# Two-level Strassen products in four stretches instead of two, with a ring of seven weight places

## The chip, the cores and the metric

The kernel runs on one core of a Trainium2 chip. The metric is the device time of one execution in microseconds (us). Lower is better.

## What is computed

One layer of a decoder trunk on 1024 tokens of width 1024, all in fp32, with two branches that share one input projection, and a final norm:

```python
h = rms_norm(x, norm_mix_g[i])
proj = jnp.einsum('bsd,dc->bsc', h, w_in[i])
(q, k, v, z_a, gk_low, cb, cc, xc, z_c, g_a, g_c) = jnp.split(proj, idx, axis=-1)
gk = jax.nn.log_sigmoid((jnp.einsum('bsr,rk->bsk', gk_low, w_gk2[i]) + b_gk[i])) / GATE_NORMALIZER
o = gla_chunked(q, k, v, gk)                       # by heads; causal gated linear attention
o = rms_norm(o, gla_norm_g[i])
y_a = jnp.einsum('bsv,vd->bsd', o * jax.nn.silu(z_a), w_branch_a[i])
u = causal_dwconv(cc * xc, conv_w[i])
y_c = jnp.einsum('bsc,cd->bsd', (cb * u) * jax.nn.silu(z_c), w_branch_c[i])
merged = jax.nn.sigmoid(g_a + b_ga) * y_a + jax.nn.sigmoid(g_c + b_gc) * y_c
x = x + jnp.einsum('bsd,de->bse', merged, w_out[i])
ple_gate = jax.nn.sigmoid(jnp.einsum('bsd,de->bse', rms_norm(x, norm_ple_g[i]), w_ple_gate[i]))
x = x + ple_gate * jnp.einsum('bsq,qd->bsd', p[i], w_ple_proj[i])
return rms_norm(x, norm_final_g)
```

q and k have 512 columns each; v, z_a, cb, cc, xc, z_c, g_a and g_c have 1024. The change touches how the projections q, k, cc, xc, z_c and cb are multiplied.

## The kernel before, in words

**Arithmetic.** Every fp32 operand is split into a high part, rounded by a ScalarE copy, and a low part, the difference that VectorE subtracts (`split`, line 598). A product of two such operands takes three matmuls, high x high, high x low and low x high (`mm3`, line 609).

**First level.** A `Cell` (line 738) is 256 columns of a weight against all 1024 tokens, cut into 2 x 2 blocks of 512 tokens or inner rows and 128 columns. It is computed with seven block products instead of eight (Strassen's scheme in Winograd's form; products 0 to 6). A first-level product is 12 matmuls of 128 x 512 into one PSUM bank. Its banks are called X, Y and V (`bank`, line 635); X holds product 0, and a copy of X by ScalarE is the seed of Y, so that product 2 adds to it. V holds product 1. The left operand of a product, the prepared weights, lies in one place of a ring of `RING` places (tiles whi and wlo); the right operand is one of seven resident sums of h (`hres`, tiles h0 to h6, high and low).

**Second level.** A `Deep` (line 855) takes two Cells a and b, whose names join to the name of its tiles (`cc2xc20` is the Deep of cc2 and xc2 for first-level product 0). It computes first-level product k (0 or 1) of both Cells together by a second seven-product scheme. Each of these second-level products is six matmuls of 128 x 256 into one half of a bank of a or b (`product`, line 900), 42 in all in place of 2 x 24 of that width. There are 17 Deeps: for k = 0 of two pairs of q and k (q0/k0, q1/k1) and eight conv pairs (cc/xc, zc/cb in four groups), and for k = 1 of seven conv pairs. `prep` (line 872) makes their weights: the sums s1 to s4 of columns of a and b, then four places of the ring by `put`: A (a11 and a12), S (s1, s2), T (s3, s4) and B (a22). The right operands are quarters of h0 (k = 0) or h1 (k = 1), and four quarter sums, "turned", that are loaded from DRAM (tqd) by `quarters` (line 1679).

**How a Deep ran.** In two stretches (`run`, line 909). The first: products 2, 1, 4 and 0, 24 matmuls, into b left, b right, a right and a left. Behind it ScalarE copies b left into a tile `dw`, VectorE adds a left to it, writes b right + dw into b left, adds a right to dw, ScalarE copies dw into a right, and VectorE adds dw to b right. The second stretch, 18 matmuls, adds products 6, 3 and 5 to b left, a left and a right. Then for k = 0 the bank becomes the Cell's X, and for k = 1 its V; for pairs that have no Deep for k = 1, and for those of k = 1, Y is then taken and seeded by a copy of X.

**What sets the order.** `line_up` (line 943) writes the order of the first-level products by hand and inserts the stretches of the Deeps between them, so that about one first-level product or more stands between two stretches of one Deep. `run_groups` (line 972) walks through this list and looks ahead: it loads weights for up to RING + 6 places and prepares them for up to RING - 1. The joint products of v and z (`joint`, line 1294; j0, j1) and the rest of these projections (`rest_of`, line 1334; tiles vY, vX) put their operands in the same ring. Work beside the products (weights of the later layers, gates) is woven in: a generator advances by `tick`, which the products call. `weights` (line 1375) loads pieces of the two later weights (tile wt), scales those of the second by a vector on ScalarE, forms the four differences of the scheme on VectorE (128 x 256 each) and stores them.

Everything is recorded by a class `Flow`, given due times from TensorE's order backwards (`set_dues`, line 373), listed per engine with a cost model (`put_in_order`, line 420), and emitted from one place, so that all instructions carry line 508 in the profile and are told apart by their tiles. TensorE follows the written order of the products; VectorE's, ScalarE's, GpSimd's and SyncE's (SP's) orders come from the list.

Of the kernel before, what the change touches and what calls it, by code (L numbers as in the profile page):

```python
# [9 lines left out]
F32 = mybir.dt.float32  # L10
# [4 lines left out]
ALU = mybir.AluOpType  # L15

P = 128
# [5 lines left out]
CH = 64  # L23
NP = HALF // P
EPS = 1e-6
RING = 8

# [490 lines left out]
def kernel(  # L520
# [16 lines left out]
    nc = Flow(tc)  # L537
    PS = bass.MemoryType.PSUM
    tt = nc.vector.tensor_tensor
# [95 lines left out]
    def bank(cell, n):  # L635
        return psm.tile([P, 512], F32, tag=f"m{3 * cell.set + n}", name=f"{cell.name}{'XYV'[n]}")
# [218 lines left out]
    class Deep:  # L855
# [53 lines left out]
        def run(self, k):  # L909
            self.prep(k)  # L910
            a, b = self.pair
            left, right = slice(0, 256), slice(256, 512)
            if k == 0:
                self.a, self.b = bank(a, 2 * self.k), bank(b, 2 * self.k)
                self.product(2, self.b[:, left], True)
                self.product(1, self.b[:, right], False)
                self.product(4, self.a[:, right], True)
                self.product(0, self.a[:, left], False)
                d = self.pool.tile([P, 256], F32, tag="dw", name=f"{a.name}{self.k}dw")
                nc.scalar.copy(d, self.b[:, left])  # L920
                tt(d, self.a[:, left], d, op=ALU.add)
                tt(self.b[:, left], self.b[:, right], d, op=ALU.add)
                tt(d, self.a[:, right], d, op=ALU.add)
                nc.scalar.copy(self.a[:, right], d)
                tt(self.b[:, right], self.b[:, right], d, op=ALU.add)
            else:
                self.product(6, self.b[:, left], False)
                self.product(3, self.a[:, left], False)
                self.product(5, self.a[:, right], False)
                for c, t in ((a, self.a), (b, self.b)):  # L930
                    if self.k:
                        c.V = t
                        c.c22 = c.taken("s5", t)
                    else:
                        c.X = t
                    if c.prods[1] == 5:
                        if c.Y is not None:
                            c.join()
                    elif self.k or 1 not in c.deep:
                        c.Y = bank(c, 1)  # L940
                        nc.scalar.copy(c.Y, c.X)

    def line_up(groups):
        for n, g in enumerate(groups):
            for s, c in enumerate(g):
                c.set = (s if len(g) > 1 else n) % 2
        todo = []
        for g in groups:
            own = [(g[s], k) for s, k in (g[0].order or [(s, k) for k in g[0].prods for s in range(len(g))])]
            if g[0].deep and g[0].prods[1] == 5:  # L950
                own.insert(3, (g[0].deep[0], 0))
                own.insert(6, (g[0].deep[0], 1))
            elif g[0].deep and 1 not in g[0].deep:
                todo.insert(len(todo) - 1, (g[0].deep[0], 0))
                own.insert(1, (g[0].deep[0], 1))
            elif g[0].deep:
                at = len(todo)
                g[0].deep[1].behind = [(c, j) for c, j in todo[-2:] if j == 6]
                for m, (k, n, left) in enumerate(((0, 0, 5), (0, 1, 3), (1, 0, 2), (1, 1, 0))):
                    todo.insert(at - left + m, (g[0].deep[k], n))  # L960
            todo += own
        return todo

# [113 lines left out]
    with phase("prep0") as pool:  # L1077
# [86 lines left out]
        at = [0]  # L1164
# [210 lines left out]
    def weights(pool, some, pace, hurry):  # L1375


        def soon(do, *a, **kw):
            nc.hurry = hurry
            do(*a, **kw)  # L1380
            nc.hurry = 0.0

        for w, kt, cs in some:
            t = pool.tile([P, 4, 256], F32, tag="wt", name=f"wt{w}_{kt}_{cs.start}")
            soon(load, t, wb[w][:, :, kt, cs].rearrange("n p c -> p n c"))
            yield pace
            b11, b12, b22, b21 = (t[:, n] for n in range(4))
            if w:
                for n, q in enumerate((b11, b12, b22, b21)):
                    k = kt + 4 * (n >= 2)  # L1390
                    soon(act, q, q, AF.Copy, scale=gple[:, k:k + 1])
                    if n != 1:
                        soon(store, wtd[w][4 + (n + 1) // 2][:, kt, cs], q)
            soon(tt, b11, b12, b11, op=ALU.subtract)
            yield 1
            soon(tt, b12, b22, b12, op=ALU.subtract)
            yield 1
            soon(tt, b22, b22, b11, op=ALU.subtract)
            yield 1
            soon(tt, b21, b21, b22, op=ALU.subtract)  # L1400
            for n, q in enumerate((b11, b22, b12, b21)):
                soon(store, wtd[w][n][:, kt, cs], q)
            yield 2
# [816 lines left out]
```

## Time and profile before

| | |
|---|---|
| median of 3 runs | 1067.74 us (1067.62 to 1067.81) |
| profiled execution, its own time | 1068.09 us |
| its span in the trace | 1066.3 us |
| instructions in the span | 15934 |
| mean granted TensorE clock | 0.998 |
| moved by DMA | 254.72 MB, mean 239 GB/s |

The profile shows one execution. Its time of 1068.09 us holds the span of 1066.3 us, first to last instruction, and 1.8 us around it. PE is TensorE, PEld its weight loads, DVE is VectorE, ACT is ScalarE, POOL is GpSimd, SP is SyncE, which issues the DMAs. In a row of the timeline the first number is the start in us, the second the duration; a bracket at the end holds the time that the engine waited before it, and for whom. In a list of waits the numbers are the sum in us, the count and the mean. In a table of windows each engine's busy time stands with its instructions, in the order PE, PEld, DVE, ACT, POOL, then the granted clock, the share of DMA and GB/s (after the window and its length).

### The profile page before, as it was taken

The numbers are of one execution on the slowest core, as the hardware profiler recorded it, in microseconds if no ns is written. First come the engines' busy times: TensorE is split into PE (matmuls) and PEld (weight loads), VectorE is DVE, ScalarE is ACT, GpSimd is POOL, SyncE is SP. The second block draws the span as 40 slices with busy tenths as digits, with TensorE's granted clock in tenths as the row PEclk, the third lists the DMA queues.
The fourth block names the chain that finished last, engine by engine and source line by source line (L and its number), as shares of the span: only waits on it lengthen the run. The fifth ranks groups of instructions, "written<-read, shape, count | busy, mean of one in ns | idle before, by whom it ended". The sixth has DMA issues, their size and how long they took to land.

```text
span 1066.3 us, 15934 instructions
## 1 busy us (share of the span) xinstructions
PE 1057.2 (99%) x5163; PEld 894.8 (84%) x5163; DVE 929.3 (87%) x1578; ACT 672.3 (63%) x1264; POOL 46.5 (4%) x83
## 2 busy tenths in 40 slices
PE   9999999999999999999999999999999999999997
PEld 7888888888888888888888888988888888888886
DVE  6899859978997889889879799996999879889896
ACT  6867859895544545656456488875856534466555
POOL 0000000000000000000000011110000000012021
PEclk9999999999999999999999999999999999999999
DMA  8997368866865544653644759868695779799953
GB/s 317 336 353 260 136 218 278 308 230 223 268 186 207 189 158 144 222 178 133 217 154 159 245 177 311 269 238 303 217 314 208 286 223 310 247 319 341 310 217 145
DMA packets 163331, 254.72 MB, mean 239 GB/s; under 512 B 14384, under 2 KB 75568, under 8 KB 160304
## 3 DMA queue, kind: packets, MB, share of 16 engines
q1 hardware_dynamic: 163104, 253.45, 70.0%
q8 instruction: 40, 0.66, 0.3%
q14 instruction: 43, 0.35, 0.1%
q10 hardware_dynamic: 144, 0.26, 0.1%
HBM read 165.58 MB, written 88.08 MB: 238 GB/s over the span
## 4 chain that ended last, share of the span: by engine, by line
PE 92%; ACT 2%; DVE 2%; DMA 2%; issue 0%; SPq 0%; POOL 0%; POOLq 0%; ACTq 0%
PE vY L508 3%; PE pe L508 2%; PE op L508 2%; PE j0Y L508 1%; PE j1X L508 1%; PE j0X L508 1%; PE j0V L508 1%; PE kv L508 1%; ACT L508 1%; DMA k0raw<-in_wc_dram 1%; PE ga1Y L508 1%; PE ga3Y L508 1%; PE k0Y L508 1%; PE cc3Y L508 1%; PE ga0Y L508 1%; PE cc2Y L508 1%
## 5 line engine op out<-in xcount | busy, mean ns | idle before, releaser
L508 ACT ACT_TABLE_LOAD x25 | 32.1, 1283 | 1.1 <-PEq L2209 0.7
L508 DVE TENSOR_TENSOR wt<-wt 128x256 f32<-128x256 f32 x64 | 27.1, 423 | 1.2 <-DMA ccd<-c 0.5
L508 ACT ACTIVATE junk<-x 128x512 bf16<-128x512 f32 (+1 forms) x30 | 18.0, 600 | 12.2 <-DVE x L508 11.9
L508 DVE SCALAR_TENSOR_TENSOR u<-t,vec,u 128x512 f32<-128x512 f32 x32 | 24.1, 753 | 0.1
L508 POOL MEMSET t<- 128x2 f32 x8 | 0.8, 99 | 399.6 <-ACT kk L508 192.9
L508 POOL TENSOR_SCALAR rg<-ms 128x1 f32<-128x1 f32 x8 | 6.4, 796 | 263.0 <-ACT junk L508 262.9
L508 ACT ACTIVATE wt<-wt,vec 128x256 f32<-128x256 f32 x32 | 13.9, 499 | 1.5 <-DMA cb2raw<-in_wc_dram 1.0
L508 ACT ACTIVATE u<-t,vec 128x512 f32<-128x512 f32 x16 | 11.6, 724 | 5.1 <-DVE t L508 4.7
L508 ACT ACTIVATE junk<-op 128x256 bf16<-128x256 f32 x32 | 12.3, 383 | 3.3 <-PE op L508 3.1
L508 ACT ACTIVATE og<-op,or 128x256 f32<-128x256 f32 x32 | 13.4, 470 | 1.0 <-POOL or L508 1.0
L508 ACT ACTIVATE oq<-oq,vec 128x512 f32<-128x512 f32 x20 | 13.2, 714 | 0.0
L508 PE MATMUL op<-v,aTh 128*128 128x256 f32 x64 | 12.8, 283 | 0.0
L508 PE MATMUL pe<-wpelo,pThi 128*128 128x512 f32 x32 | 12.8, 400 | 0.0
L508 PE MATMUL pe<-wpehi,pThi 128*128 128x512 f32 x32 | 12.7, 396 | 0.0
L508 DVE TENSOR_TENSOR s<-y,s 128x512 f32<-128x512 f32 x16 | 11.0, 687 | 1.5 <-ACT s L508 1.0
L508 POOL TENSOR_SCALAR or<-oms 128x2 f32<-128x2 f32 x16 | 6.4, 400 | 135.1 <-ACT junk L508 135.1
L508 POOL TENSOR_TENSOR or<-or,mhalf 128x2 f32<-128x2 f32 x16 | 12.2, 764 | 1.3
L508 PE MATMUL pe<-wpehi,pTlo 128*128 128x512 f32 x32 | 12.1, 394 | 0.0
L508 DVE TENSOR_TENSOR x<-x,pe 128x512 f32<-128x512 f32 (+1 forms) x18 | 11.3, 631 | 0.4
L508 DVE TENSOR_TENSOR szl<-og,szl 128x512 f32<-128x512 f32 x16 | 11.0, 686 | 0.5 <-ACT og L508 0.5
L508 DVE STREAM_TRANSPOSE oT<-szl 128x512 f32<-128x512 f32 x16 | 11.3, 707 | 0.0
L508 DVE SCALAR_TENSOR_TENSOR hq<-hq,vec,rt 128x512 f32<-128x512 f32 x16 | 11.3, 745 | 0.0
(4072 smaller groups left out, 4353.5 us busy)
## 6 DMA issues: line engine op xcount, KB each, us to landing
wtd<-wt SPq DMA_DIRECT2D x88, 128.0 KB, 2.4
wt<-in_wb_dram SPq DMA_DIRECT2D x16, 512.0 KB, 4.2
wgq<-wtd SPq DMA_DIRECT2D x7, 1024.0 KB, 7.4
vraw<-in_wv_dram SPq DMA_DIRECT2D x24, 256.0 KB, 4.4
zraw<-in_wv_dram SPq DMA_DIRECT2D x20, 256.0 KB, 3.7
uq<-ud SPq DMA_DIRECT2D x5, 1024.0 KB, 7.5
oq<-od SPq DMA_DIRECT2D x5, 1024.0 KB, 6.3
qk<-qkd SPq DMA_DIRECT2D x12, 384.0 KB, 5.1
```

The source lines that it names most:

```text
L508: o.call(*[place(a) for a in o.args], **{k: place(a) for k, a in o.kw.items()})
```

## The change

The Deep runs in four stretches: product 0; products 4 and 2; product 1; products 3, 5 and 6. Product 0 goes into a left, and ScalarE copies it into b left. Product 2 adds to this copy by TensorE, and product 1 adds to the sum. Between them ScalarE copies b left to a tile dw0 and a right to a tile dw1, and VectorE adds dw0 to a right. After product 1 VectorE writes b left + dw1 to b right. So two additions of 256 columns by VectorE and three copies by ScalarE (seed, dw0, dw1) stand where there were four additions and two copies. For k = 1 the seed of Y by a copy of X moves ahead of the last stretch. `line_up` puts one first-level product between two stretches of a Deep; where a pair has Deeps for both k, the last stretch of k = 0 and the first of k = 1 stand together. The ring has seven places instead of eight, which also shortens the reach of `run_groups` by one. In `weights`, two subtractions of 256 columns become one of 512; the woven order goes on by two steps behind it, as it did behind the two.

```diff
@@ -23,7 +23,7 @@
-RING = 8
+RING = 7
@@ -912,21 +912,26 @@
             left, right = slice(0, 256), slice(256, 512)
             if k == 0:
                 self.a, self.b = bank(a, 2 * self.k), bank(b, 2 * self.k)
-                self.product(2, self.b[:, left], True)
-                self.product(1, self.b[:, right], False)
-                self.product(4, self.a[:, right], True)
-                self.product(0, self.a[:, left], False)
-                d = self.pool.tile([P, 256], F32, tag="dw", name=f"{a.name}{self.k}dw")
-                nc.scalar.copy(d, self.b[:, left])
-                tt(d, self.a[:, left], d, op=ALU.add)
-                tt(self.b[:, left], self.b[:, right], d, op=ALU.add)
-                tt(d, self.a[:, right], d, op=ALU.add)
-                nc.scalar.copy(self.a[:, right], d)
-                tt(self.b[:, right], self.b[:, right], d, op=ALU.add)
+                self.product(0, self.a[:, left], True)
+                nc.scalar.copy(self.b[:, left], self.a[:, left])
+            elif k == 1:
+                self.product(4, self.a[:, right], False)
+                self.product(2, self.b[:, left], False)
+                self.d = [self.pool.tile([P, 256], F32, tag=f"dw{n}", name=f"{a.name}{self.k}dw{n}") for n in range(2)]
+                nc.scalar.copy(self.d[0], self.b[:, left])
+                nc.scalar.copy(self.d[1], self.a[:, right])
+                tt(self.a[:, right], self.a[:, right], self.d[0], op=ALU.add)
+            elif k == 2:
+                self.product(1, self.b[:, left], False)
+                tt(self.b[:, right], self.b[:, left], self.d[1], op=ALU.add)
+                if self.k:
+                    for c in self.pair:
+                        c.Y = bank(c, 1)
+                        nc.scalar.copy(c.Y, c.X)
             else:
-                self.product(6, self.b[:, left], False)
                 self.product(3, self.a[:, left], False)
                 self.product(5, self.a[:, right], False)
+                self.product(6, self.b[:, left], False)
                 for c, t in ((a, self.a), (b, self.b)):
                     if self.k:
                         c.V = t
@@ -936,7 +941,7 @@
                     if c.prods[1] == 5:
                         if c.Y is not None:
                             c.join()
-                    elif self.k or 1 not in c.deep:
+                    elif 1 not in c.deep:
                         c.Y = bank(c, 1)
                         nc.scalar.copy(c.Y, c.X)
 
@@ -948,16 +953,19 @@
         for g in groups:
             own = [(g[s], k) for s, k in (g[0].order or [(s, k) for k in g[0].prods for s in range(len(g))])]
             if g[0].deep and g[0].prods[1] == 5:
-                own.insert(3, (g[0].deep[0], 0))
-                own.insert(6, (g[0].deep[0], 1))
+                for n, m in enumerate((3, 5, 7, 9)):
+                    own.insert(m, (g[0].deep[0], n))
             elif g[0].deep and 1 not in g[0].deep:
-                todo.insert(len(todo) - 1, (g[0].deep[0], 0))
-                own.insert(1, (g[0].deep[0], 1))
+                at = len(todo)
+                for n in range(3):
+                    todo.insert(at - 3 + 2 * n, (g[0].deep[0], n))
+                own.insert(1, (g[0].deep[0], 3))
             elif g[0].deep:
                 at = len(todo)
                 g[0].deep[1].behind = [(c, j) for c, j in todo[-2:] if j == 6]
-                for m, (k, n, left) in enumerate(((0, 0, 5), (0, 1, 3), (1, 0, 2), (1, 1, 0))):
+                for m, (k, n, left) in enumerate(((0, 0, 5), (0, 1, 4), (0, 2, 3), (0, 3, 2), (1, 0, 2), (1, 1, 1), (1, 2, 0))):
                     todo.insert(at - left + m, (g[0].deep[k], n))
+                own.insert(1, (g[0].deep[1], 3))
             todo += own
         return todo
 
@@ -1391,10 +1399,8 @@
                     soon(act, q, q, AF.Copy, scale=gple[:, k:k + 1])
                     if n != 1:
                         soon(store, wtd[w][4 + (n + 1) // 2][:, kt, cs], q)
-            soon(tt, b11, b12, b11, op=ALU.subtract)
-            yield 1
-            soon(tt, b12, b22, b12, op=ALU.subtract)
-            yield 1
+            soon(tt, t[:, 0:2], t[:, 1:3], t[:, 0:2], op=ALU.subtract)
+            yield 2
             soon(tt, b22, b22, b11, op=ALU.subtract)
             yield 1
             soon(tt, b21, b21, b22, op=ALU.subtract)
```

How the instructions stand, at three places. In these rows every instruction carries line 508; operation, written and read tiles and the shape follow.

TensorE around the first Deep, q0/k0 (q0V is a bank of the Cell q0; k0X and q0X are the two banks of the Deep, turned0 the loaded quarter sums of h0, and q0k00 with A or S its weights), before:

```order
L508 MATMUL q0V<-h5hi,q0lo 128x512
L508 MATMUL k0X<-turned0h,q0k00Shi 128x256
L508 MATMUL k0X<-turned0l,q0k00Shi 128x256
L508 MATMUL k0X<-turned0h,q0k00Slo 128x256
L508 MATMUL k0X<-turned0h,q0k00Shi 128x256
```

and now:

```order
L508 MATMUL q0V<-h5hi,q0lo 128x512
L508 MATMUL q0X<-h0hi,q0k00Ahi 128x256
L508 MATMUL q0X<-h0lo,q0k00Ahi 128x256
L508 MATMUL q0X<-h0hi,q0k00Alo 128x256
L508 MATMUL q0X<-h0hi,q0k00Ahi 128x256
```

The Deep began with a product that reads the loaded sums; it begins with product 0, which reads a quarter of h0.

ScalarE ahead of the joint of the v products (j1c and j1V: results and banks of the joint product j1; v_1hi, v_2hi: high halves of operands of v; vY: banks of the next product), before:

```order
L508 CAST v_1hi<-vraw_1_1269 128x512
L508 COPY j1V_1396<-j1c_1451 128x512
L508 CAST v_2hi<-vraw_2_1274 128x512
L508 COPY j1V_1404<-j1c_1457 128x512
L508 COPY j1c_1553<-j1Y_1394 128x512
```

and now:

```order
L508 CAST v_1hi<-vraw_1_1274 128x512
L508 COPY j1V_1386<-j1c_1442 128x512
L508 COPY j1c_1548<-j1Y_1384 128x512
L508 COPY j1c_1552<-j1Y_1391 128x512
L508 COPY vY_1559<-j0c_1015 128x512
```

With one place fewer, the cast v_2hi and the copy of the second j1V stand behind the copies of j1Y.

ScalarE in the pair cc2/xc2 (cb1, zc1: Cells before it; s_0_1: a gate; wt: later weights; cc2X, xc2X: the banks of the Deep; cc20dw: its dw), before:

```order
L508 CAST cb1hi<-cb1T_4813 128x512
L508 CAST zc1hi<-zc1T_4633 128x512
L508 ACTIVATE s_0_1_4933<-zc1u_4818 128x512
L508 COPY cc20dw<-xc2X 128x256
L508 CAST cb1hi<-cb1T_4664 128x512
L508 ACTIVATE wt_1_0_4901<-wt_1_0_4901,vec 128x256 x4
L508 COPY cc2X<-cc20dw 128x256
```

and now:

```order
L508 CAST cb1hi<-cb1T_4833 128x512
L508 COPY xc2X<-cc2X 128x256
L508 ACTIVATE s_0_1_4913<-zc1u_4758 128x512
L508 CAST zc1hi<-zc1T_4622 128x512
L508 COPY cc20dw_4946<-cc2X 128x256
L508 CAST cb1hi<-cb1T_4637 128x512
L508 COPY cc20dw_4957<-xc2X 128x256
```

The second copy waited for a VectorE addition; now three copies wait for TensorE alone, and the scaling of wt stands behind them.

## The prediction

> **What bounds the kernel now.** I read the page first, then the waits of TensorE, then the timeline of TensorE at the places that the waits name, then the stretch that the change touches.
>
> ```profile
> span 1066.3 us, 15934 instructions
> PE 1057.2 (99%) x5163; PEld 894.8 (84%) x5163; DVE 929.3 (87%) x1578; ACT 672.3 (63%) x1264; POOL 46.5 (4%) x83
> PE 92%; ACT 2%; DVE 2%; DMA 2%; issue 0%; SPq 0%; POOL 0%; POOLq 0%; ACTq 0%
> ```
>
> TensorE is busy for 1057.2 of 1066.3 us, and the chain that ended last runs over it for 92%. A busy TensorE can still hide waits, since matmuls overlap in the records, so the list of its own waits counts for more:
>
> ```profile
> PE warm L508 <- DVE zero L508: 1.0, 1, 1.0
> PE q0X L508 <- DMA turned0l<-tqd_0l: 0.3, 1, 0.3
> PE vY L508 <- ACT vY L508: 0.2, 1, 0.2
> ```
>
> That is the whole list: 1.0 us at the start and two waits later. The last matmul starts here:
>
> ```profile
> 1058.40 0.28 PE L508 MATMUL gt3Z<-wg6hi,gt3lo 128*128 128x256 f32 x1
> ```
>
> It ends at 1058.7, so the tail behind TensorE is 7.6 us. The order of its last rows on VectorE and ScalarE is unchanged, so I price it at nothing. The stretch that the change rewrites lies within 238 to 590 us:
>
> ```profile
> 290.00:590.00 300.00, 300.00 (x1619) 260.88 (x1619) 264.33 (x512) 162.51 (x326) 1.35 (x10) 1.00 0.54 178
> ```
>
> TensorE is busy for all 300 us of it, at the full granted clock (1.00), VectorE for 264 (88%), ScalarE for 163 (54%). So work taken off VectorE is taken off an engine that TensorE does not wait for. What can be gained is the two waits; what can be lost is any new wait in 17 products, or TensorE's own handling of a finer cut. A measurement of this kernel tells about 0.2%, 2.1 us, from no change.
>
> **What leaves VectorE.**
>
> ```profile
> 445.86 0.42 DVE L508 TENSOR_TENSOR cc20dw<-cc2X,cc20dw 128x256 f32<-128x256 f32 x1
> 446.19 0.42 DVE L508 TENSOR_TENSOR cc2xc21S<-xc2T 128x256 f32<-128x256 f32 x1
> 446.52 0.43 DVE L508 TENSOR_TENSOR xc2X<-xc2X,cc20dw 128x256 f32<-128x256 f32 x1
> L508 DVE TENSOR_TENSOR wt<-wt 128x256 f32<-128x256 f32 x64 | 27.1, 423 | 1.2 <-DMA ccd<-c 0.5
> ```
>
> Additions of 256 columns follow each other every 0.33 us. 17 products lose two each: 34 x 0.33 = 11.2 us. Of the 64 subtractions for the later weights, 16 pairs become 16 of twice the width; that saves at most 16 x 0.33 = 5.3, and next to nothing if one of 512 takes the 0.69 of the row of cc2xc21Tlo below. ScalarE gets one copy more per product, 17 x 0.38 = 6.5 us (its row is below). All of it lies beside a TensorE that waits for neither: worth 0 on the path.
>
> A rule speaks for more. The Trainium skill, page "Perfetto Trace Analysis", section "Identifying the Most-Contended Engine", holds that matmul busy time says little of TensorE's headroom and that the busy share of its weight loads does. Here that is 84%, less than VectorE's 87%; by it VectorE would be the one to relieve, and the sum would fall by the 11 us above. The list of waits disagrees: after the start TensorE waited for VectorE not once.
>
> **The first second-level product (q0, k0).** Its matmuls were held up by the loads of the quarter sums:
>
> ```profile
> 234.08 0.43 SPq L508 DMA_DIRECT2D turned0l<-tqd_0l  x1
> 238.09 0.28 PE L508 MATMUL k0X<-turned0h,q0k00Shi 128*128 128x256 f32 x1
> 240.32 0.39 PE L508 MATMUL q0X<-turned0l,q0k00Shi 128*128 128x256 f32 x1 [0.27 <-DMA turned0l<-tqd_0l]
> 241.74 0.40 PE L508 MATMUL k0V<-h5hi,k0hi 128*128 128x512 f32 x1
> 442.31 0.28 PE L508 MATMUL xc2X<-turned0h,cc2xc20Shi 128*128 128x256 f32 x1
> 445.18 0.40 PE L508 MATMUL cb1V<-h5hi,cb1hi 128*128 128x512 f32 x1
> turned0l<-tqd_0l SPq DMA_DIRECT2D x1, 256.0 KB, 6.2
> ```
>
> The 24 matmuls take 241.74 - 238.09 = 3.65 us here and 445.18 - 442.31 = 2.87 where nothing waits: 0.78 lost. A matmul of 256 columns takes 2.87 / 24 = 0.12.
>
> The first stretch now reads h0, which lies on chip, and a first-level product of 2.7 us stands before the first use of turned0. The sums tqd_0 are also loaded first instead of last. The last load landed at 234.08 + 6.2 = 240.28; the stretch that needs a loaded sum begins at about 238.09 + 6 x 0.12 + 2.75 = 241.6, and the sum loaded last is needed one product later still. I take the whole 0.78 away: **-0.8** (bounds -0.8 and 0, if another late load takes the place of this one).
>
> **Seven places at the joint of the v products.** In ScalarE's order, ahead of the vY copies that TensorE waits for, two instructions went behind the j1c copies: the v_2hi cast and the copy of the second j1V.
>
> ```profile
> 130.25 0.62 ACT L508 CAST v_1hi<-vraw 128x512 fp32r<-128x512 f32 x1 [0.73 <-PE j1V L508]
> 131.80 0.62 ACT L508 CAST v_2hi<-vraw 128x512 fp32r<-128x512 f32 x1
> 132.84 1.06 ACT L508 COPY j1c<-j1Y 128x512 f32<-128x512 f32 x2
> ...
> 131.41 0.39 PE L508 MATMUL j1Y<-j141hi,qs1h 128*128 128x512 f32 x1
> 133.91 0.39 PE L508 MATMUL vY<-v_0hi,h2lo 128*128 128x512 f32 x1
> 134.45 0.50 PE L508 MATMUL vY<-v_0hi,h2hi 128*128 128x512 f32 x1 [0.16 <-ACT vY L508]
> 134.78 0.39 PE L508 MATMUL vY<-v_0lo,h2hi 128*128 128x512 f32 x1
> ```
>
> The stall is (134.45 - 133.91) + (134.78 - 134.45) less two steps of 0.23: 0.4 us. With one place fewer the v_1hi cast waits for a later product, whose last matmul starts at 131.41, so the cast starts at 131.6 rather than 130.25; cast and copy, at my estimate of 0.52 each from the two j1c copies in 1.06, put the j1c copies at 132.65, 0.2 earlier than 132.84. **-0.2** (bounds -0.4 and 0).
>
> **The finer cut on TensorE.** The work is the same 42 matmuls per product, but the order shows 61 unbroken runs of them where there were 34. What a run costs its successor, from the chain that ended last and the timeline:
>
> ```profile
> 445.34 2.75 PE cb1V L508 x12
> 452.96 2.75 PE cb1Y L508 x12
> 254.99 2.72 PE k0X L508 x12
> ```
>
> The twelve matmuls of 512 columns behind a run (24 and 18 long: the first two rows) take 2.75 us, those in mid-row (k0X) 2.72. If each of the 27 new runs costs the same 0.03, that is 27 x 0.03 = **+0.8**. The new runs are of 6 and 12, which the trace does not have, so the bounds are 0 and 0.8; I take the nearest rows, those of 18.
>
> **The new waits: ScalarE between the stretches.** After the first stretch ScalarE copies one half bank to the other bank (the seed), after the second it copies both (dw); TensorE comes back after one first-level product, 2.72 to 2.75 us. In ScalarE's order of the pair cc2/xc2, the chain that ended in a copy behind VectorE became three copies that wait for TensorE alone; the scaling of weights (wt), which waits for a load, went behind them.
>
> ```profile
> 443.94 0.38 ACT L508 COPY cc20dw<-xc2X 128x256 f32<-128x256 f32 x1
> 444.59 0.62 ACT L508 CAST cb1hi<-cb1T 128x512 fp32r<-128x512 f32 x1 [0.28 <-PE cc2X L508]
> 446.18 1.71 ACT L508 ACTIVATE wt<-wt,vec 128x256 f32<-128x256 f32 x4 [0.97 <-DMA cb2raw<-in_wc_dram]
> ...
> L508 ACT ACT_TABLE_LOAD x25 | 32.1, 1283 | 1.1 <-PEq L2209 0.7
> ```
>
> Behind the second stretch stand a cast (0.62) and a copy (0.38): 1.0 us, with handovers some 1.2, against 2.75. Both cases of k fit; where a table load (1.28, last row above) stands between, 2.5. Behind each waiting copy ScalarE queues the next casts; these have one product more. VectorE's first addition (a right + dw0) must be done ahead of the last stretch: 2.72 + 0.72 + 2.72 = 6.2 us after its input. The second reads b left, which the last product of that stretch overwrites: 2.72 + 2 x 0.72 = 4.2 us. Behind them on VectorE wait low halves of weights with 3 us to spare (below). Priced at 0; without that cover, its price is the first rival.
>
> **The ring of seven.** The tightest weights before are the second of two products in a row:
>
> ```profile
> 452.72 0.69 DVE L508 TENSOR_TENSOR cc2xc21Tlo<-cc2xc21S,cc2xc21Thi 128x512 fp32r<-128x512 f32 x1
> 456.51 0.28 PE L508 MATMUL xc2V<-turned1h,cc2xc21Tlo 128*128 128x256 f32 x1
> ```
>
> Done at 453.41, used at 456.51: 3.1 us. One place fewer frees each about one product, 2.72 us, later, which leaves 0.4; but the stretches now need A alone at first, S after another product and T after two, which gives back 2.7 to 5.4. So 0, bounds 0 and the second rival.
>
> **Sum.** The profiled execution took 1068.09 us (span 1066.3 and 1.8 around it), 0.35 above the median 1067.74 of the three. 1068.09 - 0.8 - 0.2 + 0.8 = 1067.9, and against the median 1067.74 - 0.2 = **1067.5 us**. Ends of the terms: 1067.74 - 1.2 = 1066.5 and 1067.74 + 0.8 = 1068.5.
>
> **Rivals.** (1) ScalarE is late: its queue holds casts that wait for weights' places, and 2.75 us don't cover it. Decides where more than 1.5 us stand ahead of the last dw copy beyond those I counted. At 0.5 us in each of 17 products: 1067.5 + 8.5 = 1076. Against it: ScalarE is 54% busy there, and waited for TensorE. Chance 0.05. (2) Seven places are too few: VectorE, 88% busy, fills a place late, and the 0.4 us left by the sizes above are used up. Seven pairs of products at 0.5 us: +3.5, 1071. It decides from 0.4 us of delay beyond the place lost. Chance 0.05. (3) VectorE was the bound after all, hidden in modelled matmul ends: 11 us off, 1056.5. TensorE's list of waits speaks against it, since no wait on VectorE stands in it after the start; the busy shares of 84% and 87% speak for it. Chance 0.03. The rule named above points to this case. (4) One wait of up to 2 us at q0/k0 or elsewhere in place of those removed: up to 1069.5. Chance 0.07, and no difference. The forecast keeps 0.80.
>
> **Chances.** Slower by over 0.2% (above 1069.9) 0.10, from 1 and 2; faster (below 1065.6) 0.03, from 3; within 0.87. The range reaches from the best ends, 1066.4, into case 4, 1069.0.
>
> **What would show it.** Right: no wait of TensorE on turned0; 24 matmuls of a first product without the 0.78; products behind the short runs at 2.75; VectorE busy 11 to 20 us less (34 rows of 0.42, and what the wide subtractions save) with the span unchanged. Wrong: TensorE idle behind a copy of a dw or X tile (rival 1) or behind a low half of A, S, T (rival 2); a span shorter by 10 us (rival 3); products behind the short runs at 2.72, which would make it 0.8 less.

## The result and the profile after

Over 22 runs each, the changed kernel takes 1069.39 us (median; 1069.06 to 1070.04) and the kernel before 1068.39 (1067.32 to 1069.33). The ratio is 1.0013 with a 95% interval of 1.0007 to 1.0019: 1.0 us slower, which is within 0.2%. The range of the prediction, 1066.4 to 1069.0, does not hold 1069.39.

The head of the page of the changed kernel: span, busy times, and the chain that ended last.

```profile
span 1067.3 us, 15920 instructions
PE 1057.8 (99%) x5163; PEld 894.5 (84%) x5163; DVE 920.0 (86%) x1528; ACT 674.7 (63%) x1277; POOL 43.8 (4%) x83
PE 98%; ACT 1%; DMA 0%; DVE 0%; issue 0%; POOL 0%; POOLq 0%; ACTq 0%
```

VectorE does 50 instructions and 9.3 us less. TensorE does the same 5163 matmuls, and the span is 1.0 us longer. TensorE's whole list of waits:

```profile
PE warm L508 <- DVE zero L508: 1.0, 1, 1.0
PE q0X L508 <- ACT q0u L508: 0.4, 1, 0.4
```

The wait on turned0 is gone; a wait on q0u is new. q0u is ScalarE's copy of q0's X, taken behind the last stretch of the first Deep. TensorE's and, in the second fence, ScalarE's timeline at that place:

```profile
250.72 0.28 PE L508 MATMUL k0X<-h0hi,q0k00Blo 128*128 128x256 f32 x1
251.36 0.50 PE L508 MATMUL q0X<-h3hi,q0hi 128*128 128x512 f32 x1 [0.36 <-ACT q0u L508]
251.70 0.39 PE L508 MATMUL q0X<-h3lo,q0hi 128*128 128x512 f32 x1
```

```profile
250.20 0.62 ACT L508 CAST q1k10Thi<-q1k10S 128x512 fp32r<-128x512 f32 x1
250.73 0.58 ACT L508 COPY q0u<-q0X 128x512 f32<-128x512 f32 x1
```

The next product of the order adds to the same bank, X of q0. It must wait until q0u has read it, and q0u stands behind a cast of weights. The steps of TensorE are 0.64 and 0.34 where 0.12 and 0.23 would do: 0.63 us lost.

The rest of the loss has no wait beside it. In the chain that ended last, twelve matmuls of 512 columns behind second-level products that read quarter sums take 2.76 us. Ahead of zc1Y the rows of cc2X and xc2X are products 4 and 2, one run of twelve; ahead of cb1Y xc2X is product 1, a run of six:

```profile
445.97 0.72 PE cc2X L508 x6
446.69 0.72 PE xc2X L508 x6
447.41 2.76 PE zc1Y L508 x12
450.17 0.72 PE xc2X L508 x6
450.89 2.76 PE cb1Y L508 x12
```

To see all of it at once I took the starts of the 5163 matmuls and subtracted, within each stage, 0.2267 us for a matmul of 512 columns, 0.1197 for 256 and 0.109 for 128. What is left is time that TensorE lost. In us, for one profiled execution each ("start" is from the first matmul to the end of the first product, pe; "v, z" from the joint products j0 to the first q matmul; "later" are all other projections up to zc3; "tail" runs from the start of the last matmul to the end of the span):

| kernel | start | v, z | q0/k0 | later | rest | tail | span |
|---|---|---|---|---|---|---|---|
| before | 2.77 | 1.02 | 0.85 | 0.73 | 0.80 | 7.91 | 1066.31 |
| after | 2.37 | 0.89 | 0.87 | 1.93 | 0.81 | 8.26 | 1067.35 |
| after, again (e5) | 2.99 | 0.88 | 0.87 | 1.92 | 0.80 | 8.29 | 1067.99 |

The two executions of the changed kernel agree to 0.03 us in every stage, but for the start, which differs by 0.6. So the change is, without the start: -0.13 in v and z, +0.02 at q0/k0 (-0.78 for turned0, +0.63 for q0u, the rest for the finer cut), **+1.20** in the later projections, and **+0.35** in the tail. The sum is 1.44. The medians differ by 1.0 to 1.2, and the interval of the ratio, 0.7 to 2.0 us, holds 1.44; what the 0.2 to 0.4 between them is was not found.

About 0.3 of the 0.6 in the start is a load: ScalarE's cast of pThi, an operand of the first product, waits 1.51 us for the load of pTraw in e5 and 0.49 in the other trace, and the matmuls behind it lose 0.33 more. The rest lies in TensorE's first dozen steps, most of them 0.43 us in place of 0.23. The Trainium skill, "TensorE: Matmul & The Clock Gate", section "Part 1: The HAM clock gate (the "warmup" mystery)", holds that the time until the full clock is granted differs from run to run, since its window runs freely. No trace here shows this: the granted clock reads 1.00 from the first 2 us on in both executions.

For the narrow runs the same reckoning, by the length of the run: its own steps and those of the twelve matmuls behind it, in us for all runs of that length (the waits at q0/k0 left out):

| kernel | 6 | 12 | 18 | 24 or 30 | sum |
|---|---|---|---|---|---|
| before | | | 17: 0.46 | 17: 0.41 | 34: 0.87 |
| after | 27: 0.99 | 17: 0.76 | 10: 0.27 | 7: 0.21 | 61: 2.23 |

The finer cut costs 1.36 us, 0.05 for each of 27 new runs. With unrounded starts and 0.1197 the two sums come to 0.79 and 2.18, and the difference to 1.39.

### The profile page after: what moved, and what is told of

It reads as the page before. It is cut to its first block, busy times and chain, and to the rows that moved or that the text cites. A ratio compares the mean times of both kernels' runs of the same rounds, so it can differ in the third digit from the quotient of the medians.

```text
span 1067.3 us, 15920 instructions
## 1 busy us (share of the span) xinstructions
PE 1057.8 (99%) x5163; PEld 894.5 (84%) x5163; DVE 920.0 (86%) x1528; ACT 674.7 (63%) x1277; POOL 43.8 (4%) x83
## 4 chain that ended last, share of the span: by engine, by line
PE 98%; ACT 1%; DMA 0%; DVE 0%; issue 0%; POOL 0%; POOLq 0%; ACTq 0%
PE zY L508 3%; PE vY L508 3%; PE pe L508 2%; PE op L508 2%; PE j0Y L508 1%; PE zV L508 1%; PE j1V L508 1%; PE j1X L508 1%; PE j0V L508 1%; PE j0X L508 1%; PE kv L508 1%; PE xc3Y L508 1%; PE cb1Y L508 1%; PE cb0Y L508 1%; PE cb2Y L508 1%; PE xc1Y L508 1%
## 5 line engine op out<-in xcount | busy, mean ns | idle before, releaser
L508 DVE TENSOR_TENSOR wt<-wt 128x256 f32<-128x256 f32 (+1 forms) x48 | 24.4, 509 | 0.2
L508 ACT CAST S<-S 128x512 fp32r<-128x512 f32 (+1 forms) x18 | 10.2, 569 | 2.5 <-PE op L508 2.1
```

Of the source, the lines that this page charges most:

```text
L508: o.call(*[place(a) for a in o.args], **{k: place(a) for k, a in o.kw.items()})
```

## The experiments

My theory (A): the cut itself costs this, and neither the ring, nor VectorE, nor ScalarE's new copies. Rival B: ring and copies cost it. Rival C: VectorE sets the pace. Differences are to the kernel before on the same chip, unless said otherwise.

**The cut without the new sums (e1).** The kernel before, with the changed kernel's `line_up`, and

```diff
+            elif k == 1:
                 self.product(1, self.b[:, right], False)
                 self.product(4, self.a[:, right], True)
+            elif k == 2:
                 self.product(0, self.a[:, left], False)
```

and the seed of Y moved as in the change.

> The kernel before, with its four additions and eight ring places, but its Deeps cut into four stretches (2 | 1, 4 | 0 and the additions | 6, 3, 5) at the places that the changed kernel uses. Theory A (the finer cut itself costs: in the trace of the changed kernel the 61 runs of narrow matmuls lose 2.2 us where the 34 before lost 0.85): 27 new runs at 0.05 us = +1.35, turned0 stall of 0.78 gone, a wait of the product behind q0/k0 on the copy q0u new at 0.6 to 0.9: +1.2 to +1.5 us over the kernel before. Theory B (the cost is the ring of seven and the new ScalarE copies): the stall of 0.78 goes, 0.6 to 0.9 comes, no more: -0.2 to +0.2.

Measured: 1085.84, ratio 1.0164 (1.0150 to 1.0178), far beyond both. TensorE waits on VectorE in 12 of the 17 Deeps; the first three rows of the waits' list:

```profile
PE xc3X L508 <- DVE xc3X L508: 1.3, 1, 1.3
PE q0X L508 <- ACT q0u L508: 1.1, 1, 1.1
PE xc2X L508 <- DVE xc2X L508: 1.1, 1, 1.1
```

The old chain of copy, four additions and copy was hidden by two first-level products; here one stands between. So the runs' cost can't be read from this time. In the trace it can: the 17 runs of 12 lose 0.76 as in the changed kernel, and the ten runs of six that read quarter sums (product 2) lose 0.044 behind them. Of the 17 runs of six that read h (product 0) three have no wait behind them; they lose 0.026 to 0.028. So it is the cut, not the new sums. And at these places the old additions come too late.

**The ring alone (e2), the wide subtraction alone (e3).**

```diff
-RING = 8
+RING = 7
```

> The kernel before with seven ring places in place of eight and nothing else. Theory A: within 0.3 us of the kernel before, TensorE waits as before. Theory B: +0.7 to +1.2 us, with waits of TensorE on low or high halves of weights.

```diff
-            soon(tt, b11, b12, b11, op=ALU.subtract)
...
-            soon(tt, b12, b22, b12, op=ALU.subtract)
...
+            soon(tt, t[:, 0:2], t[:, 1:3], t[:, 0:2], op=ALU.subtract)
```

> The kernel before with only the two subtractions of later weights made into one of 512 columns. Theory A (VectorE is not waited for): within 0.3 us of the kernel before, VectorE busy a few us less. Theory C (VectorE is the engine that sets the pace, so work taken off it is worth its time): 2 us or more faster.

Measured: 1067.62, ratio 0.9993 (0.9985 to 1.0002), and 1067.50, 0.9993 (0.9984 to 1.0002): 0.6 and 0.7 us less, which neither theory had said, though the intervals reach 1. The stage table shows where: q0/k0 0.07 and 0.08 in place of 0.85. The loads of turned0 on SyncE's queue in e3, first and last (231.28 and 234.08 before):

```profile
225.93 0.40 SPq L508 DMA_DIRECT2D turned0h<-tqd_1h  x1
...
228.27 0.43 SPq L508 DMA_DIRECT2D turned0l<-tqd_0l  x1
```

They are issued over 5 us earlier, in e2 some 4: any edit ahead of it lists the stage anew. So the stall that I priced at 0.78 is real, and each of two side edits takes it away alone. Rival B, as far as the ring goes, and rival C fall: the later stage is at 0.74 and 0.72 as before, and no 2 us are won. ScalarE's new copies, the other part of B, show no wait in the list above.

**The first Deep earlier (e4).**

```diff
-                for n, m in enumerate((3, 5, 7, 9)):
+                for n, m in enumerate((2, 4, 6, 8)):
...
-                yield 1
+                if k:
+                    yield 1
```

> The changed kernel with the four stretches of the first Deep q0/k0 one first-level product earlier (places 2, 4, 6, 8 in place of 3, 5, 7, 9; its quarter sums are recorded without pauses). Theory A: the wait of q0X on the copy q0u (0.63 us with its slower step) goes, and the sums land in time or nearly: 0.3 to 0.65 us faster than the changed kernel, so +0.4 to +0.8 over the kernel before. Rival: the sums of turned0 come late again at the second stretch, and the wait moves to turned0: no faster than the changed kernel, +1.0 or more.

Measured: 1069.51, ratio 1.0011 (1.0003 to 1.0020): no faster than the changed kernel, as the rival had it, but not by its mechanism. The wait on q0u is gone and none on turned0 came; q0/k0 falls from 0.87 to 0.23. The same edit lists v and z anew, where two steps of zY lose 0.25 (1.16 in place of 0.88), and the tail is 0.1 longer. The 0.3 that should be left of the 0.64 is not to be seen in the medians: 0.1 less than e5, 0.1 more than the first 22 runs.

**The changed kernel again (e5), and operands from h alone (e6).** The edit of e6, in `quarters`:

```diff
-            turned[k].extend([b11, t3, t2, b21, t1, b22, t4])
+            b12 = at(hi, 0, 1), at(lo, 0, 1)
+            turned[k].extend([b11, b12, b22, b21, b12, b22, b11])
```

> The changed kernel once more, unchanged, to stand beside the three below on one chip, and to see which parts of its trace are the same in every execution. Theory A: the steps behind the narrow runs (2.2 us in 61 runs) and the wait on q0u (0.36 shown, 0.63 with its slower steps) come again to 0.05 us; the first 50 us of the program, which differ by up to 1 us between the traces so far, do not. Rival: the narrow runs' losses vary as the start does, and are noise.

> The changed kernel with the quarter sums (turned0, turned1) replaced by quarters of h0 and h1 as the right operands of the second-level products, so that part of the computation is another one; the loads still run. Theory A1 (a run costs what its last products' operands make it: 0.028 behind a quarter of h, 0.044 behind quarter sums): all 61 runs cost 0.028, the sum falls from 2.2 to 1.7 us less the runs' own gains, so 0.4 to 0.6 us under the changed kernel. Theory A2 (a run costs by its length, short ones 0.044): the rows stay at 0.044 and the time stays.

Measured: e5 1069.59, ratio 1.0012 (1.0003 to 1.0021), its runs 0.99, 0.76, 0.27 and 0.21, the same to 0.01. e6 1068.49, 1.0003 (0.9994 to 1.0012): 1.1 us under e5. All its 61 runs lose 0.028 behind them, and the sum is 1.50 in place of 2.23; the tail is 7.95 in place of 8.29. So 0.7 of the 1.1 is what quarter sums cost as operands, and 0.34 is the tail. Length alone (A2) is out.

**The old kernel's first stretch reordered (e7, and again as e11).**

```diff
+                self.product(0, self.a[:, left], True)
                 self.product(2, self.b[:, left], True)
                 self.product(1, self.b[:, right], False)
-                self.product(4, self.a[:, right], True)
-                self.product(0, self.a[:, left], False)
+                self.product(4, self.a[:, right], False)
```

> The kernel before with the first stretch in the order 0, 2, 1, 4 in place of 2, 1, 4, 0, so that the quarter sums are needed 0.7 us later and the long run of 24 ends in three products that read them. Theory A1: the 24-runs cost 0.045 in place of 0.028, 17 x 0.017 = +0.3; the turned0 stall (0.78 where an execution has it) goes: -0.5 to +0.3 against the kernel before. Theory A2: the 24-runs stay at 0.028, -0.8 to 0.

> The kernel before with the first stretch in the order 0, 2, 1, 4, once more: the losses behind its narrow runs (24 long: -0.016 or +0.004 each) come again to 0.005, if they are a matter of the order of operands and not of the execution; rival: they are 0.03 as in the kernel before.

Measured: 1067.60, ratio 0.9994 (0.9985 to 1.0003); one execution in e11, 1067.76. The runs of 24 lose nothing: -0.15 in sum in e11, -0.016 and +0.004 each in both. A1 had 0.045 and A2 0.028, so both simple rules fall: the last operand doesn't decide either. Where TensorE waits, the two executions of this kernel differ: e7 loses 0.17 more at q0/k0, where a load of turned0 is still late, and e11 0.15 more in v and z, at two steps of zY.

**Three stretches (e8).** Product 1 moves to the head of the last stretch, and `line_up` has three places per Deep:

```diff
-            elif k == 2:
-                self.product(1, self.b[:, left], False)
-                tt(self.b[:, right], self.b[:, left], self.d[1], op=ALU.add)
+            else:
...
-            else:
+                self.product(1, self.b[:, left], False)
+                tt(self.b[:, right], self.b[:, left], self.d[1], op=ALU.add)
                 self.product(3, self.a[:, left], False)
```

The quarter sums of h0 are recorded without pauses, as in e4.

> The changed kernel with product 1 put at the head of the last stretch: three stretches (0 | 4, 2 | 1, 3, 5, 6), 44 runs in place of 61, and the first Deep's early enough that nothing waits on q0u. Theory A: the runs lose about 1.55 us in place of 2.2, the q0u wait of 0.63 goes: 1.0 to 1.4 us under the changed kernel, at the kernel before or up to 0.4 over it. Rival (VectorE must now add b left to b right within the 1.44 us of products 3 and 5, and comes late): 0.2 to 0.5 us of wait in each of 17 Deeps, 3 to 8 us over the changed kernel.

Measured: 1069.41, ratio 1.0009 (1.0001 to 1.0018), 0.2 under e5. The runs lose 1.50 as expected (44 of them), q0/k0 is at 0.15. But VectorE is late once, as the rival had it for all 17:

```profile
PE xc3X L508 <- DVE xc3X L508: 0.5, 1, 0.5
PE zY L508 <- ACT zu L508: 0.3, 1, 0.3
```

The first costs 0.77 with its slower steps, the second, in a stage listed anew, 0.5 (v and z 1.44 in place of 0.88).

**The tail (e9).** Behind the last DMA SyncE runs its closing row. By the trace, a gap of 0.33 to 0.35 us stands in it where SyncE has 1492 to 1495 instructions: behind the row's fifth at 1492 (e4, e7), the fourth at 1493 (after, e5), the second at 1495 (e8). In all of these it stands ahead of SyncE's 1488th instruction. At 1479 and 1501 (e3, e2) there is none, and the tail is 7.9. At 1490 (before) a gap of 0.36 stands ahead of the 1488th as well, but the row's last gap is 0.15 there in place of 0.38, and the tail is 7.9. The edit:

```diff
+            if k:
+                for m in range(8):
+                    load(cp.tile([P, 64], F32, name=f"spare{m}"), vecs)
```

> The changed kernel with eight small loads more, of 32 KB each, issued by SyncE in the middle of the program into tiles that nobody reads. In the traces so far the time behind the last matmul is 7.9 us where SyncE has 1479, 1490 or 1501 instructions and 8.2 to 8.4 where it has 1492 to 1495; there a gap of 0.33 to 0.35 us stands in SyncE's closing row, one place earlier for each instruction more. Theory T (the gap stands at a fixed count of SyncE's instructions): with some 1501 the gap leaves the closing row, the tail is 7.9 us and the time 0.35 us under the changed kernel. Rival (it belongs to the new order of the Deeps): the tail stays at 8.26.

Measured: 1069.21, ratio 1.0010 (1.0001 to 1.0019). With 1501 instructions the gap is gone. The span and the last matmul's and last DMA's rows of the changed kernel, and then of e9:

```profile
span 1067.3 us, 15920 instructions
...
1059.09 0.28 PE L508 MATMUL gt3Z<-wg6hi,gt3lo 128*128 128x256 f32 x1
1063.18 0.40 ACTq L508 DMA_DIRECT2D out_dram<-x  x1
```

```profile
span 1067.4 us, 15927 instructions
...
1059.46 0.28 PE L508 MATMUL gt3Z<-wg6hi,gt3lo 128*128 128x256 f32 x1
1063.56 0.39 ACTq L508 DMA_DIRECT2D out_dram<-x  x1
```

Both issue the last DMA 4.1 us behind the last matmul; then 4.2 us follow in the one and 3.8 in the other. Theory T holds in the trace (7.92 for 8.26). In the medians e9 is 0.2 to 0.4 under the changed kernel (1069.39 and 1069.59), too little to tell by themselves. The traces show more: in all 20 of them a gap of 0.33 us or more stands ahead of SyncE's 80th, 208th, 336th instruction and so on, every 128th, and the 1488th is one of this series. With 1497 instructions (e18) it meets the head of the closing row, and the tail is 8.26.

**Which property of the quarter sums (e10, e13, e14, e15, e17, and e16 timed).** Their order within the tiles (e10); product 1 alone from h (e13); both tiles further on by unused space (e14, e16: 640 bytes, e17: 128); high and low tile 512 bytes further apart (e15):

```diff
-                th, tl = (tq.tile([P, 3, 2, 256], F32R, name=f"turned{k}{w}") for w in "hl")
+                th, tl = (tq.tile([P, 2, 3, 256], F32R, name=f"turned{k}{w}") for w in "hl")
...
-                back.append((th[:, n], tl[:, n]) if n < 3 or k else (at(hi, 0, 1), at(lo, 0, 1)))
+                back.append((th[:, :, n], tl[:, :, n]) if n < 3 or k else (at(hi, 0, 1), at(lo, 0, 1)))
```

turned1 is changed in the same way.

> The changed kernel with the quarter sums stored in another order in their tiles (inner row first, then the sum), so that two inner rows of a sum lie 3 KB (turned0) or 4 KB (turned1) apart in place of 1 KB; in h0 and h1 they lie 2 KB apart. Theory L (the place of the operand's rows makes the 0.044 behind short runs that read quarter sums): these rows fall to 0.028 as with quarters of h, 0.6 to 0.8 us under the changed kernel. Rival (it is not the stride): they stay at 0.044 and the time stays within 0.3.

```diff
-            turned[k].extend([b11, t3, t2, b21, t1, b22, t4])
+            turned[k].extend([b11, b22, t2, b21, t1, b22, t4])
```

> The changed kernel with the right operand of second-level product 1 alone replaced by a quarter of h, so that part of the computation is another one; products 4 and 2 still read quarter sums. If what a run reads itself decides (theory A1), the 17 runs of product 1 fall from 0.043 to 0.028 each behind them, and the 17 runs of products 4 and 2 stay at 0.044. Rival (what the whole Deep reads, or a state kept over first-level products, decides): both change or neither.

```diff
+            if k == 0:
+                load(cp.tile([P, 160], F32, name="pad")[:, 0:32], vecs[:, 0:32])
```

> The changed kernel with 640 bytes per partition of unused space (and one small load) ahead of the tiles of the quarter sums, so that both lie 640 bytes further on. Theory L2 (their place against boundaries of the memory makes the 0.044): the rows behind runs that read them change by 0.005 or more. Rival: they stay.

```diff
-                th, tl = (tq.tile([P, 3, 2, 256], F32R, name=f"turned{k}{w}") for w in "hl")
+                th, tl = (tq.tile([P, 1664], F32R, name=f"turned{k}{w}")[:, 0:1536].rearrange("p (n m c) -> p n m c", n=3, m=2) for w in "hl")
```

turned1 is lengthened in the same way.

> The changed kernel with the high and the low tile of the quarter sums 512 bytes further apart (each tile is that much longer). Theory L3 (the distance between the high and the low operand, which alternate from matmul to matmul, makes the 0.044): the rows behind runs that read them change by 0.005 or more. Rival: they stay.

The edit of e16 is that of e14, and of e17 that with 32 in place of 160 columns:

> The changed kernel with 640 bytes per partition of unused space once more, timed. The trace of its first run lost 1.5 us less than the changed kernel behind and in its matmuls (0.5 in the products of v and z, 1.0 in the later projections), at a tail of 8.37 in place of 8.26. If the place of the operands in memory makes this: 1.2 to 1.5 us under the changed kernel, that is within 0.4 of the kernel before, and the same steps again to 0.05. Rival (one execution's luck): as the changed kernel, 1.0 to 1.3 over the kernel before.

> The changed kernel with 128 bytes of unused space in place of 640. 2048 bytes more (e9) and 512 bytes more between the high and the low tile (e15) changed nothing. If 512 is a whole step of what matters, 128 does what 640 did: 0.028 or less behind the runs that read quarter sums, and 1.5 us less lost. Rival (640 is near a boundary that 128 does not reach): 0.044 as in the changed kernel.

Measured, with the runs' loss from the traces:

| kernel | us | runs of 6 | of 12 | all 61 | v, z | later | tail |
|---|---|---|---|---|---|---|---|
| after | 1069.39 | 0.99 | 0.76 | 2.23 | 0.89 | 1.93 | 8.26 |
| e10 | 1069.64, 1.0013 (1.0004 to 1.0022) | 0.99 | 0.76 | 2.23 | 0.89 | 1.93 | 8.29 |
| e13 | 1068.88, one execution | 0.60 | 0.76 | 1.84 | 0.88 | 1.58 | 7.93 |
| e15 | 1069.94, one execution | 0.99 | 0.76 | 2.23 | 0.88 | 1.93 | 8.30 |
| e16 | 1068.08, 1.0002 (0.9993 to 1.0011) | 0.46 | 0.33 | 1.18 | 0.37 | 0.95 | 8.36 |
| e17 | 1068.09, one execution | 0.46 | 0.33 | 1.18 | 0.39 | 0.95 | 8.35 |

e14, one execution of the same kernel as e16, gave 1067.83 and the same steps to 0.01. What a run reads itself decides (e13: product 1's runs change, those of 4 and 2 don't). A stride of 3 or 4 KB in place of 1 (e10) changes nothing, nor do 512 bytes more between high and low (e15). But a shift of the tiles by 128 or 640 bytes takes 1.5 us away, all of it without a wait. A shift of 2048 bytes (e9, whose spare tiles lie in the same pool) changed nothing. This fits 512 bytes as a whole step. If it is one, e10 and e15 moved by whole steps alone and could not show an effect: stride and distance are open for other sizes. The unused space moves every tile behind it, not the quarter sums alone. But the runs of product 0, which read h0 and weights of the same ring, lose 0.028 behind them in e16 as before, so the runs that changed changed by what they read. Behind a run of product 1 the loss falls from 0.044 to 0.028 (turned0) and from 0.043 to 0.015 (turned1). The same chain as above in e16:

```profile
445.07 0.71 PE cc2X L508 x6
445.78 0.72 PE xc2X L508 x6
446.50 2.75 PE zc1Y L508 x12
449.25 0.71 PE xc2X L508 x6
449.96 2.75 PE cb1Y L508 x12
```

The half us in v and z comes from the 40 matmuls of the gates that are woven in (lowp and zp, 0.27) and from the twelve steps behind them (0.21). The weights of lowp (glx) lie in a later pool and moved too. In the changed kernel, then in e16:

```profile
155.89 0.40 PE L508 MATMUL lowp<-h0hi,glx 128*128 128x512 f32 x1
...
157.28 0.40 PE L508 MATMUL lowp<-h0hi,glx 128*128 128x512 f32 x1
```

```profile
156.02 0.39 PE L508 MATMUL lowp<-h0hi,glx 128*128 128x512 f32 x1
...
157.38 0.39 PE L508 MATMUL lowp<-h0hi,glx 128*128 128x512 f32 x1
```

Six steps take 1.39 us in the one and 1.36 in the other.

**What the gains make together (e12, e18).** e12 is e7 with e3's subtraction; e18 has seven places and the 640 bytes as well.

> The kernel before with the first stretch in the order 0, 2, 1, 4 and the two subtractions of later weights made one. If the parts add up as the traces say (turned0 stall of 0.78 gone by either, 0.5 less behind the runs of 24), 1.2 us under the kernel before, less 0.35 to 0.45 if the gap falls into SyncE's closing row: -0.8 to -1.2. Rival: the gains of the two singly (0.8 and 0.9) are one and the same stall, and nothing more: -0.7 to -0.8.

> The kernel before with the first stretch in the order 0, 2, 1, 4, the subtractions of later weights made one, seven ring places and the 640 bytes of unused space. If the gains add up: as e12 (1.0 under the kernel before) and 0.5 more in the products of v and z: 1.2 to 1.7 us under the kernel before. Rival (the order 0, 2, 1, 4 lost nothing already, and the place of v and z differs with seven places): as e12, 0.8 to 1.1 under.

Measured: e12 1067.31, ratio 0.9989 (0.9981 to 0.9998); e18 1067.22, 0.9992 (0.9983 to 1.0001). e12 is faster than both kernels, by 1.0 us than before: q0/k0 -0.02, later 0.27, tail 7.92 with 1482 instructions on SyncE. In e18, v and z fall to 0.51, but the runs lose 0.50 (e11: 0.31), since the order 0, 2, 1, 4 lost little already, and with 1497 instructions the tail is 8.26. It adds nothing that can be measured: 0.8 under the kernel before, at the low end of what the rival had. With the shift, the runs of 24 that end in quarter sums of h0 lose 0.027 behind them, where they lost nothing in e11.

## Why the prediction was wrong

The forecast was 0.2 us less; the measured difference is 1.0 us more. The term of the finer cut was mis-sized (1.36 for 0.8), and two new delays were put at nothing: a wait on q0u (0.63) and a longer tail (0.35). Term by term:

- **The base.** 1067.74 was the median of three runs; 22 runs give 1068.39. This is 0.65 of the 1.9 us between 1067.5 and 1069.39. The difference forecast was -0.2, the measured one is +1.0. Three executions don't fix a median where the start alone differs by 0.6.
- **Term -0.8, turned0.** The size was right (e2, e3: 0.78 gone). The step "**The new waits**" failed beside it: I checked the cover between stretches, and not what follows the last one. X of q0 goes straight into the next product, so the copy q0u stands on the path: +0.63. Rival 4 had described such a wait, at 0.07 and up to 1069.5, but the range ended at 1069.0. Nor does the stall's end in the changed kernel show that the new order ended it, since the ring alone and the subtraction alone end it too.
- **Term +0.8, the finer cut.** The mechanism was right, the size wrong: 1.36, above the upper bound of 0.8. The 0.03 was taken from long runs. Of the 1.36, 0.63 are the 27 runs at what they cost when they read h (e6: 1.50 - 0.87), and 0.73 are short runs that read quarter sums at their place in memory (e6, e13, e16). No row of the trace before showed it: every run there had 18 or 24 matmuls and ended in a quarter of h0 or h1. The bound needed room above, not only below.
- **Term -0.2, v and z.** It is -0.13 in the stage, of the right sign. At the joint itself, where the term was worked out, it is -0.07: the two steps of vY lose 0.43 before and 0.35 after. The rest is spread over v and z.
- **The tail at 0.** Its rows on VectorE and ScalarE are indeed unchanged; SyncE's closing row was left out: +0.35 (e9).
- **VectorE at 0 and the ring at 0.** Right: 9.3 us less VectorE brought nothing (I said 11 to 20 less), and no wait on weights appeared. The rule of the Trainium skill, page "Perfetto Trace Analysis", section "Identifying the Most-Contended Engine", by which VectorE would have been the one to relieve if the weight loads' busy share is taken for TensorE, does not hold here: e3 won only the stall. The page names a second measure beside that share, the part of the peak arithmetic that is reached, and it was not worked out. The list of waits was the better guide.
- **ScalarE's copies between the stretches at 0.** Right: no wait on a dw or a seed stands in the list.

Terms by the trace: -0.78 + 0.63 - 0.13 + 1.36 + 0.35 = 1.43, the sum of the stages but for 0.01.

Open: which addresses cost, and whether 512 bytes is the step; why the order 0, 2, 1, 4 loses nothing with no space put in, though its last products read quarter sums. And the kernel before with the shift alone was not run.

## What to carry to other kernels

Here one engine was busy for 99% and its list of waits held 1.5 us; work taken off the others bought nothing, and the finer interleaving was paid for on the busy engine. So price each switch by rows of the very length and operands that it will have, or leave the bound open above. Follow each moved step to the first reader behind its end, not only to its own next stage. Differences of 0.1% want more than three runs of the base, and a table of lost time by stage, since starts, closing rows and places in memory move by as much.

## What the runs showed of the hardware that was not expected

- Matmuls of 256 columns whose right operand (quarter sums) lies at one place cost up to 0.044 us behind a run of six; 128 or 640 bytes further on 0.028 or 0.015, with no wait. Matmuls of 512 with weights at one place took 0.232 a step, and 0.227 shifted (six steps of 1.39 and 1.36). In all 1.5 us of 1069.
- A gap of 0.33 us or more stands ahead of every 128th of SyncE's instructions (the 80th, 208th and so on) in all 20 traces. Where the 1488th falls into the closing row, at 1492 to 1497 instructions, the tail is 8.2 to 8.4 us in place of 7.9. What makes the gap was not tried.
- Two executions of the changed kernel differ by 0.6 us in the first 30 us, and by 0.03 or less in every later stage. Where TensorE waits on a load or a copy, two executions differed by 0.17 (q0/k0, e7 and e11).
